# Strassen pairs of a two-layer encoder: where the weight block sums are formed, and the order of the seven products

## The chip, the core and the metric

The kernel runs on one core of one Trainium2 chip. A core has a matrix engine (TensorE, PE in the profile), three engines for elementwise work (VectorE or DVE, ScalarE or ACT, GpSimd or POOL), a sequencer that only issues transfers (SP), and 16 DMA engines that move data between the chip's main memory and the core's on-chip buffers. Each engine works through its own queue in order; semaphores make one wait for another. The metric is the device time of one execution in microseconds (us), the median of several runs.

## What is computed

Two layers over 528 tokens (16 learned meta tokens, then 512 grid tokens) of width 2048, in float32. Each begins with an RMS norm and a large input projection and ends with an output projection added to the residual:

```python
def even_layer(h, ...):
    u = rmsnorm(h, norm_g)
    proj = einsum("bld,de->ble", u, w_in)            # 2048 -> 12352
    y_a = ssd_mixer(...)                             # bidirectional state-space heads
    y_b = conformer_conv(...) * silu(z_b)            # 31-tap convolution channels
    return h + einsum("ble,ed->bld", concat([y_a, y_b]), w_out)   # 4096 -> 2048

def odd_layer(h, ...):
    u = rmsnorm(h, norm_g)
    q, k, v, z = split(einsum("bld,de->ble", u, w_in))            # 2048 -> 8192
    o = neighbourhood_attention(q, k, v, rpb)
    return h + einsum("ble,ed->bld", o * silu(z), w_out)          # 2048 -> 2048
```

A final RMS norm follows, and the meta tokens are dropped.

## The kernel before

Activations are kept transposed: a tile holds 128 channels by 528 tokens. A weight matrix is read in panels of 128 output columns; half a panel is [128 x 8 x 128] floats, 512 KB, one transfer. A float32 product is made of three faster ones: the weight is split into a high part `wh` (ACT, line 196) and a low part `wl` (DVE, line 199), the activations likewise, and each of the eight blocks of 128 rows takes three matmuls (high by high, high by low, low by high). `wh` and `wl` have three buffers each, so the split for a product can begin once the product three before it has left the PE.

Most of the output projections, and the q, k, v projection, are done by Strassen's scheme in Winograd's form. Two panels a and b are a pair; with their upper and lower halves they make the four weight blocks A11, A12 (of a) and A21, A22 (of b), the tokens are cut into two halves, and seven products of 24 matmuls replace eight. On the weights' side this needs four sums,

```python
S1 = A21 + A22;  S2 = S1 - A11;  S3 = A11 - A21;  S4 = A12 - S2
```

which `block_ops` makes on DVE (lines 163, 167, 171). On the activations' side similar combinations (`combos`) are made once a stage: `ta` for products 5 and 7, `tb` for product 6, and a fourth that goes through memory and replaces half of the plain activations for product 4. There are four stages with pairs; each begins with four plain panels (`proj`), during which the combinations are made:

- a: even layer, output projection of the state-space half, 6 pairs;
- b: its convolution half, 6 pairs, added to what a left in memory (`pt_d`);
- c: odd layer, projection to v, q, k, 22 pairs, scaled on POOL (line 823) and stored to `vqk_d`;
- d: odd layer, output projection on 512 tokens, 6 pairs, with the residual.

`sproj` runs the products of a pair: each into its own PSUM tile `pb` (four buffers), then `evac`, the merge, which adds the seven results into the four output blocks, then `fetch` for a coming product. `todo` holds one entry per half panel or product in order; a `fetch` takes the next entry, which issues its load on SP (`load`, line 144) or its sums, and splits one that is there already. Three entries are kept split ahead (`AHEAD`). The products' order is a table: "F" (1, 2, 6, 7, 5, 3, 4) for most pairs, "L" and "E" for the last pair of a stage, with merges of their own (`merge`, and `late` and `early` in stage d).

A scheduler that estimates times sets the order of the rows on each engine's queue, outside the attention part, which is ordered by hand.

Of the kernel before, what the change touches and what calls it, by code (L numbers as in the profile page):

```python
# [12 lines left out]
F32 = mybir.dt.float32  # L13
F32R = mybir.dt.float32r
AF = mybir.ActivationFunctionType
ALU = mybir.AluOpType

P = 128
# [35 lines left out]
ORD = {"F": (1, 2, 6, 7, 5, 3, 4), "L": (1, 2, 4, 3, 6, 7, 5), "E": (4, 6, 7, 5, 1, 2, 3)}  # L54
WOP = {1: "A11", 2: "A12", 3: "S4", 4: "A22", 5: "S1", 6: "S2", 7: "S3"}
NORM = 2
NORMF = 2
PRE = {"F": {0: ("A12", "A21", "A22"), 1: ("S1",)}, "L": {0: ("A12", "A21"), 1: ("S1",), 2: ("S2",)}, "E": {0: ("A21", "S1"), 1: ("S3",), 4: ("A12",)}}
# [17 lines left out]
def hybrid_encoder(ctx: ExitStack, tc: tile.TileContext, hT, win, wdt, wout, oin, oout, par, con,  # L76
# [51 lines left out]
    for seq, last in (([wout[0, (m + 2 * NORM) % KT] for m in range(KT)], "L"), ([wout[1, m] for m in range(KT)], "L"), (vqk, "E")):  # L128
        panels += seq[:2 * NORM]
        for j in range(NORM, len(seq) // 2):  # L130
            panels.append((seq[2 * j], seq[2 * j + 1], last if j == len(seq) // 2 - 1 else "F"))
    panels += [oin[48 + p] for p in range(KT)]
    panels += [oout[m] for m in range(2 * NORMF)]
    for j in range(NORMF, KT // 2):
        panels.append((oout[2 * j], oout[2 * j + 1], "E" if j == KT // 2 - 1 else "F"))
# [11 lines left out]
    def block_ops(pa, pb, order):  # L147
        b = {}

        def get(n):  # L150
            if n in b:
                return b[n]
            if n in ("A11", "A12"):
                r = load(pa, int(n[2]) - 1)
            elif n == "A21":
                r = load(pb, 0)
            elif n == "A22":
                r = load(pb, 1, wx[0], "raw2", 1)
            elif n in ("S1", "S2"):
                x, y, o = ("A21", "A22", ALU.add) if n == "S1" else ("S1", "A11", ALU.subtract)  # L160
                x, y = get(x), get(y)
                r = wx[0].tile([P, KH, P], F32, name=n, tag="sx", bufs=2)
                nc.vector.tensor_tensor(r, x, y, op=o)  # L163
            elif n == "S3":
                get("S1")
                r = get("A21")
                nc.vector.tensor_tensor(r, get("A11"), r, op=ALU.subtract)  # L167
            else:
                y = get("S2")
                r = get("A12")  # L170
                nc.vector.tensor_tensor(r, r, y, op=ALU.subtract)
            b[n] = r
            return r
# [1159 lines left out]
```

## Time and profile before

| | us |
|---|---|
| median of 3 runs | 2707.42 (2706.79 to 2709.77) |
| profiled execution | 2707.44 |
| its span, first to last instruction | 2705.7 |
| PE busy | 2630.5 (97%) |
| PE's weight loads busy | 2508.7 (93%) |
| DVE busy | 2147.2 (79%) |
| ACT busy | 1389.0 (51%) |
| POOL busy | 528.5 (20%) |

Stages a, b and c with their plain panels run from about 1310 to 2175 us, stage d from about 2520 us to the end. Read in the profile: a line of groups gives source line, engine, operation, output and input, count, busy time with the mean in ns, and the idle time of the engine just before with what ended it. A line of waits gives total us, times, and the longest. In the windows, columns are stretch, length, and for each engine busy us with the count of instructions, then the granted PE clock, the share of the DMA engines' time, and GB/s. The PE's matmuls overlap, so its busy time is not its load; the rate of matmuls is.

### The profile page before, as it was taken

How to read it: one execution, taken by the hardware profiler on the slowest of the kernel's cores; microseconds unless marked ns; L12 is line 12 of the kernel's file. 1: busy time of each engine (PE TensorE's matmuls, PEld its weight loads, DVE VectorE, ACT ScalarE, POOL GpSimd, SP SyncE). 2: the span in 40 equal slices, each digit the busy share in tenths (PEclk: the TensorE clock that was granted, in tenths of full speed). 3: DMA queues.
4: the chain of work that ended last, by engine and by line, in shares of the span. 5: the costliest groups of instructions: out<-in, count | busy, mean ns of one | idle time of the engine just before them, and what ended most of it. 6: DMA issues, size and time to landing. Idle time of an engine off the chain costs nothing.

```text
span 2705.7 us, 52618 instructions
## 1 busy us (share of the span) xinstructions
PE 2630.5 (97%) x21228; PEld 2508.7 (93%) x21228; DVE 2147.2 (79%) x2990; ACT 1389.0 (51%) x2567; POOL 528.5 (20%) x568
## 2 busy tenths in 40 slices
PE   8999999999999999999999999999999989999997
PEld 7999999999999999999999999999999967777796
DVE  7775967878587979986888888888888866666886
ACT  5355585665757655225634435533333345655543
POOL 2000000000000001101333532312212242443321
PEclk9999999999999999999999999999999989999998
DMA  4222222222222323434745746633333354444644
GB/s 161 95 76 94 84 74 94 84 94 83 79 90 78 97 77 102 151 128 149 251 141 192 232 150 217 201 130 125 129 132 126 123 154 120 124 131 131 231 161 150
DMA packets 150627, 354.51 MB, mean 131 GB/s; under 512 B 32896, under 2 KB 49408, under 8 KB 150384
## 3 DMA queue, kind: packets, MB, share of 16 engines
q1 hardware_dynamic: 143552, 328.92, 37.8%
q0 software_dynamic: 6544, 22.17, 2.3%
q8 instruction: 166, 2.72, 0.4%
q14 instruction: 77, 0.63, 0.1%
q10 hardware_dynamic: 288, 0.07, 0.0%
HBM read 300.66 MB, written 50.43 MB: 130 GB/s over the span
## 4 chain that ended last, share of the span: by engine, by line
PE 73%; DVE 8%; issue 7%; DMA 5%; ACT 4%; POOL 3%; SPq 0%; DVEq 0%; POOLq 0%; ACTq 0%
PE ps L235 38%; PE pb L216 19%; PE ps L988 7%; DVE wl L199 2%; PE po L974 2%; PE py L506 2%; PE pq L925 1%; PE st L446 1%; ACT wh L196 1%; POOL srt L782 1%; DVE a L529 1%; DVE S L163 1%; DVE raw L167 1%; DMA raw<-oout 1%; DMA raw<-oin 1%
## 5 line engine op out<-in xcount | busy, mean ns | idle before, releaser
L196 ACT ACTIVATE wh<-raw 128x1024 fp32r<-128x1024 f32 (+1 forms) x458 | 484.4, 1058 | 714.2 <-PE pb L216 282.4
L235 PE MATMUL ps<-rh,wh 128*128 128x264 f32 (+2 forms) x3536 | 739.0, 288 | 11.0 <-ACT rh L252 9.2
L235 PE MATMUL ps<-rh,wl 128*128 128x264 f32 (+2 forms) x3536 | 738.9, 288 | 0.2 <-DVE wl L199 0.2
L235 PE MATMUL ps<-rl,wh 128*128 128x264 f32 (+2 forms) x3536 | 734.9, 288 | 1.2 <-DVE rl L253 1.1
L199 DVE TENSOR_TENSOR wl<-raw,wh 128x1024 fp32r<-128x1024 f32 (+1 forms) x458 | 593.3, 1295 | 123.9 <-ACT wh L196 117.7
L235 PEld LDWEIGHTS ps<-rh,wh 128*128 128x128 f32 (+1 forms) x3536 | 554.6, 189 | 17.1 <-ACT rh L252 9.2
L235 PEld LDWEIGHTS ps<-rh,wl 128*128 128x128 f32 (+1 forms) x3536 | 554.0, 189 | 3.4 <-DVE wl L199 0.5
L235 PEld LDWEIGHTS ps<-rl,wh 128*128 128x128 f32 (+1 forms) x3536 | 551.9, 189 | 5.4 <-DVE rl L253 2.0
L216 PE MATMUL pb<-rh,wl 128*128 128x264 f32 (+1 forms) x1280 | 366.9, 287 | 8.7 <-DVE wl L199 8.4
L216 PE MATMUL pb<-rh,wh 128*128 128x264 f32 (+1 forms) x1280 | 365.1, 285 | 3.1 <-ACT wh L196 3.1
L216 PE MATMUL pb<-rl,wh 128*128 128x264 f32 (+1 forms) x1280 | 365.0, 285 | 0.0
L529 DVE SCALAR_TENSOR_TENSOR a<-up,prm,a 128x528 f32<-128x528 f32 x464 | 343.8, 770 | 2.3 <-ACT a L524 0.9
L216 PEld LDWEIGHTS pb<-rh,wl 128*128 128x128 f32 x1280 | 242.2, 189 | 12.4 <-DVE wl L199 12.2
L216 PEld LDWEIGHTS pb<-rh,wh 128*128 128x128 f32 x1280 | 243.0, 190 | 3.7 <-ACT wh L196 3.5
L216 PEld LDWEIGHTS pb<-rl,wh 128*128 128x128 f32 x1280 | 242.7, 190 | 0.0
L216 PE MATMUL pb<-ta,wh 128*128 128x264 f32 (+1 forms) x1280 | 236.4, 285 | 4.6 <-ACT wh L196 4.6
L216 PEld LDWEIGHTS pb<-ta,wh 128*128 128x128 f32 x1280 | 199.1, 189 | 5.7 <-ACT wh L196 5.7
L216 PE MATMUL pb<-ta,wl 128*128 128x264 f32 (+1 forms) x640 | 181.3, 285 | 0.6 <-DVE wl L199 0.4
L196 ACT ACTIVATE wh<-S 128x1024 fp32r<-128x1024 f32 x80 | 84.5, 1057 | 118.7 <-PE pb L216 92.1
L216 PE MATMUL pb<-tb,wh 128*128 128x264 f32 (+1 forms) x640 | 125.5, 293 | 4.4 <-ACT wh L196 3.4
L216 PEld LDWEIGHTS pb<-ta,wl 128*128 128x128 f32 x640 | 120.5, 189 | 1.5 <-DVE wl L199 1.5
L988 PE MATMUL ps<-rh,wh 128*128 128x512 f32 x272 | 114.3, 420 | 0.0
(319 smaller groups left out, 4097.6 us busy)
## 6 DMA issues: line engine op xcount, KB each, us to landing
raw<-win SPq DMA_DIRECT2D x192, 512.0 KB, 3.6
raw<-oin SPq DMA_DIRECT2D x128, 512.0 KB, 3.7
raw<-wout SPq DMA_DIRECT2D x64, 512.0 KB, 4.1
raw<-oout SPq DMA_DIRECT2D x32, 512.0 KB, 3.8
srt<-h_d SPq DMA_DIRECT2D x38, 264.0 KB, 4.6
srt<-yz_d SPq DMA_DIRECT2D x32, 264.0 KB, 4.9
srt<-yb_d SPq DMA_DIRECT2D x32, 264.0 KB, 4.2
vqk_d<-cx SPq DMA_DIRECT2D x26, 264.0 KB, 2.0
```

The costliest lines, as they stand in the source:

```text
L163: nc.vector.tensor_tensor(r, x, y, op=o)
L167: nc.vector.tensor_tensor(r, get("A11"), r, op=ALU.subtract)
L196: nc.scalar.activation(wh, raw, AF.Copy)
L199: nc.vector.tensor_tensor(wl, raw, wh.bitcast(F32), op=ALU.subtract)
L216: nc.tensor.matmul(o, w[:, k, :], u[:, lo:lo + n], start=(k == 0 and j == 0), stop=(k == KH - 1 and j == 2))
L235: nc.tensor.matmul(ps[:M, n, :N], w[:, k, :], u[:, lo + n * N:lo + (n + 1) * N], start=(kk == 0 and j == 0), stop=(kk == KT - 1 and j == 2))
L446: nc.tensor.matmul(st[:, :nd * 256], xb[:, c, 256:], xd[:, d0:d1].rearrange("p r x -> p (r x)"), start=True, stop=True)
L506: nc.tensor.matmul(py[j * HD:(j + 1) * HD, c // 3, (c % 3) * CH:(c % 3 + 1) * CH], a, b, start=(q == 0), stop=(q == nt - 1))
L529: nc.vector.scalar_tensor_tensor(a, u[:, j:j + L], wv(j), a, op0=ALU.mult, op1=ALU.add)
L782: nc.gpsimd.tensor_tensor(r, r, t, op=ALU.add)
L974: nc.tensor.matmul(self.po[hs, w * P:(w + 1) * P], lt, rt, start=(q == 0), stop=(q == nq - 1))
L988: nc.tensor.matmul(ps, w[:, k, :], u[:, lo:lo + S], start=(kk == 0 and j == 0), stop=(kk == KT - 1 and j == 2))
```

## The change

The block sums leave DVE. Two tiles per pair, `wy` (two buffers) and `wx` (one), are loaded by SP and then added to in place by transfers that POOL issues with an addition (`accum_op`): `wy` is A21, then A21 + A22 (product 5), then + A11 (product 6), then + A12 (product 3); `wx` is A11 (product 1), then + A21 (product 7). A12 (product 2) and A22 (product 4) are plain loads. Each addition is issued after the low split that last read the tile (`post`); `wy` of the next pair is started up to three entries early (`EARLY`). Every weight block is so read from memory twice. With all signs plus on the weights' side, signs on the activations' side and in the merges change to match.

The order is the same for every pair, (5, 1, 2, 6, 7, 3, 4), and three products are accumulated onto the PSUM tile of an earlier one: 6 onto 1, 3 onto 5, 4 onto 7, so a pair uses four tiles. The merges shrink: in stages a to c from seven DVE operations and one ACT copy to five and two.

```diff
-ORD = {"F": (1, 2, 6, 7, 5, 3, 4), "L": (1, 2, 4, 3, 6, 7, 5), "E": (4, 6, 7, 5, 1, 2, 3)}
+ORD = (5, 1, 2, 6, 7, 3, 4)
+BANK = {5: "c", 1: "a", 2: "b", 6: "a", 7: "e", 3: "c", 4: "e"}
...
-            elif n in ("S1", "S2"):
-                x, y, o = ("A21", "A22", ALU.add) if n == "S1" else ("S1", "A11", ALU.subtract)
-                x, y = get(x), get(y)
-                r = wx[0].tile([P, KH, P], F32, name=n, tag="sx", bufs=2)
-                nc.vector.tensor_tensor(r, x, y, op=o)
...
+    def block_ops(pa, pb):
+        s = {}
+
+        def half(a, hf):
+            return a[:, hf * KH:(hf + 1) * KH, :]
+
+        def add(n, a, hf):
+            nc.gpsimd.dma_start(s[n], half(a, hf), accum_op=ALU.add)
+
+        def start():
+            s["y"] = load(pb, 0, wx[0], "wy", 2)
+            add("y", pb, 1)
+
+        def left():
+            s["x"] = load(pa, 0, wx[0], "wx", 1)
+            return s["x"]
+
+        return [Entry(lambda: s["y"], start, lambda: add("y", pa, 0)),
+                Entry(left, None, lambda: add("x", pb, 0)),
+                Entry(lambda: load(pa, 1)),
+                Entry(lambda: s["y"], None, lambda: add("y", pa, 1)),
+                Entry(lambda: s["x"]),
+                Entry(lambda: s["y"]),
+                Entry(lambda: load(pb, 1))]
...
+    def take():
+        e = todo.popleft()
+        e.early()
+        pend.append((e.get(), e.post))
+        for e in list(todo)[:EARLY]:
+            if wx[0] is not None:
+                e.early()
...
             nc.vector.tensor_tensor(wl, raw, wh.bitcast(F32), op=ALU.subtract)
             halves.append((wh, wl, M))
+            if post:
+                post()
             if todo:
-                pend.append(todo.popleft()())
+                take()
...
-            ps = wx[1].tile([P, 512], F32, name="pb", tag="pb")
+            new = BANK[b] not in banks
+            if new:
+                banks[BANK[b]] = wx[1].tile([P, 512], F32, name="pb", tag="pb")[:, :n]
...
+                    nc.tensor.matmul(o, w[:, k, :], u[:, lo:lo + n], start=(new and k == 0 and j == 0),
+                                     stop=(k == KH - 1 and j == 2), skip_group_check=not new)
+            evac(b, o, banks)
...
-        def merge(order, x, y):
+        def merge(x, y):
+            def evac(n, p, banks):
+                if n == 1:
+                    nc.scalar.activation(x1, p, AF.Copy)
+                elif n == 2:
+                    vv(x1, x1, p, op=ALU.add)
+                elif n == 6:
+                    nc.scalar.activation(u, p, AF.Copy)
+                    vv(y2, u, banks["c"], op=ALU.add)
                 elif n == 7:
+                    st(y2, y2, -1.0, p, op0=ALU.mult, op1=ALU.subtract)
                 elif n == 3:
                     vv(x2, u, p, op=ALU.add)
+                elif n == 4:
+                    st(y1, u, -1.0, p, op0=ALU.mult, op1=ALU.subtract)
```

How this moves the rows on the engines' queues, at the three places that matter below. On DVE in the middle of stage c, before (S and raw are weight tiles of the block sums, cx, cy and u tiles of the merge):

```order
L163 TENSOR_TENSOR S_22931<-raw,raw_22898 128x1024
L740 TENSOR_TENSOR cx<-u_22769,pb 128x264
L163 TENSOR_TENSOR S_22963<-S_22931,raw 128x1024
L167 TENSOR_TENSOR raw<-raw 128x1024
L199 TENSOR_TENSOR wl<-raw,wh 128x1024
L742 TENSOR_TENSOR cy<-u_22770,pb 128x264
L199 TENSOR_TENSOR wl<-S_22963,wh 128x1024
L171 TENSOR_TENSOR raw<-raw,S_22963 128x1024
```

and now, at such a place:

```order
L203 TENSOR_TENSOR wl<-raw,wh 128x1024
L203 TENSOR_TENSOR wl<-wy,wh 128x1024
L203 TENSOR_TENSOR wl<-wx,wh 128x1024
L717 TENSOR_TENSOR cx<-cx,pb 128x264
L203 TENSOR_TENSOR wl<-wy,wh 128x1024
L203 TENSOR_TENSOR wl<-raw,wh 128x1024
L720 TENSOR_TENSOR cy<-u_23045,pb 128x264
L722 SCALAR_TENSOR_TENSOR cy<-cy,pb 128x264
```

The four sums of a pair are gone, and low splits and merge operations alone are left. On POOL in stage c, before (the scaling of the output tiles of three pairs; the numbers of the tiles are kept):

```order
L823 TENSOR_TENSOR cx_23233<-cx_23233,rs0_84 128x528
L823 TENSOR_TENSOR cy_23234<-cy_23234,rs0_84 128x528
L823 TENSOR_TENSOR cx_23466<-cx_23466,rsa_85 128x528
L823 TENSOR_TENSOR cy_23467<-cy_23467,rs0_84 128x528
L823 TENSOR_TENSOR cx_23699<-cx_23699,rs0_84 128x528
```

and now (wy_23302, wy_23528 and wy_23754 belong to three pairs that follow each other):

```order
L161 DMA wx_23428<-oin 128x1024
L806 TENSOR_TENSOR cy_23270<-cy_23270,rs0_84 128x528
L161 DMA wy_23302<-oin 128x1024
L161 DMA wy_23754<-oin 128x1024
L161 DMA wy_23528<-oin 128x1024
L806 TENSOR_TENSOR cx_23495<-cx_23495,rs0_84 128x528
L161 DMA wx_23654<-oin 128x1024
```

Four adding transfers of each pair stand between the two scalings. On PE at the first pair of stage b, now (pb_17747 is product 2, pb_17684 product 5, pb_17717 product 6 on the tile of product 1):

```order
L224 MATMUL pb_17747<-rh_17030,wh_17600 128x264
L224 MATMUL pb_17747<-rl_17031,wh_17600 128x264
L224 MATMUL pb_17747<-rh_17030,wl_17601 128x264
L224 MATMUL pb_17684<-ta0_17624,wh_17444 128x264
L224 MATMUL pb_17717<-tb0_17166,wh_17709 128x264
L224 MATMUL pb_17717<-tb1_17167,wh_17709 128x264
L224 MATMUL pb_17717<-tb0_17166,wl_17710 128x264
```

Product 5 comes first with 18 matmuls, products 1 and 2 are taken in between, and its last blocks follow here, mixed with product 6.

201 lines of the change are left out of this document (61 added, 140 removed).

## The prediction

> **What bounds the kernel now.** I read the clock first (one core, mean granted 0.986), then the windows of the four stages in which the Strassen pairs run, then what TensorE (PE) waits for there, and last the DMA view. The stages, by their matmuls at line 216, are: a, 6 pairs (first half of the even layer's output projection); b, 6 pairs (second half); c, 22 pairs (the odd layer's q, k, v projections); d, 6 pairs (the odd layer's output projection).
>
> ```profile
> core 0: us, PE busy (x) PEld busy (x) DVE busy (x) ACT busy (x) POOL busy (x), PEclk, DMA share, GB/s
> 1345.00:1481.00 136.00, 128.29 (x1009) 125.35 (x1009) 118.53 (x119) 53.04 (x65) 46.17 (x21) 0.99 0.51 165
> 1528.00:1670.00 142.00, 131.74 (x1008) 129.28 (x1007) 126.16 (x141) 64.94 (x88) 49.79 (x33) 0.95 0.55 178
> 1724.50:2174.00 449.50, 445.48 (x3613) 443.24 (x3613) 382.30 (x398) 170.75 (x185) 93.08 (x43) 1.00 0.40 132
> 2555.00:2685.50 130.50, 122.39 (x1012) 120.42 (x1010) 110.28 (x141) 58.56 (x75) 38.94 (x33) 0.99 0.46 151
> ...
> 1750.00:1800.00 50.00, 50.00 (x411) 50.00 (x411) 43.02 (x45) 18.59 (x19) 10.23 (x5) 1.00 0.40 133
> ```
>
> The last row is a stretch without a gap: 50 us / 411 = 121.7 ns a matmul. A pair has 7 products of 24 matmuls, so a product takes at least 2.92 us and a pair 20.4 us. By that measure stage a needs 6 x 20.4 = 122.6 us and took 136, so 13.4 us are lost; b lost 142 - 122.6 = 19.4 us. In c matmul records are missing, so I count its idle PE: 449.5 - 445.5 = 4.0 us. Stage d has 256 columns in place of 264, 119 us by proportion, so it lost 11.5 us. **About 48 us in all is the ceiling** of what this change can win in the pairs, since it leaves every matmul in place. What the PE waits for (stages a, b, c, d in turn):
>
> ```profile
> PE pb L216 <- DVE wl L199: 7.2, 9, 1.8
> ...
> PE pb L216 <- ACT wh L196: 6.9, 7, 2.4
> PE pb L216 <- DVE wl L199: 3.3, 2, 2.3
> ...
> PE pb L216 <- DVE wl L199: 3.8, 3, 2.5
> ...
> PE pb L216 <- ACT wh L196: 4.3, 4, 2.9
> PE pb L216 <- DVE wl L199: 3.0, 3, 1.1
> ```
>
> It waits for the split weights, and the low half comes from VectorE (DVE), which is 85 to 89% busy in all four. So DVE is the second limit; in c it just fits under the PE.
>
> **What leaves DVE.** The groups of block sums, over all 40 pairs:
>
> ```profile
> L163 DVE TENSOR_TENSOR S<-raw,raw 128x1024 f32<-128x1024 f32 x40 | 50.1, 1253 | 37.9 <-DMA raw<-oin 15.6 <-DMA raw<-wout 10.3 <-DMA raw<-oout 7.4
> L163 DVE TENSOR_TENSOR S<-S,raw 128x1024 f32<-128x1024 f32 x40 | 54.2, 1355 | 0.1
> L167 DVE TENSOR_TENSOR raw<-raw 128x1024 f32<-128x1024 f32 x40 | 81.3, 2033 | 0.0
> L171 DVE TENSOR_TENSOR raw<-raw,S 128x1024 f32<-128x1024 f32 x40 | 81.2, 2031 | 0.1
> L725 DVE TENSOR_TENSOR cx<-u,pb 128x264 f32<-128x264 f32 x33 | 13.7, 416 | 0.0
> L723 ACT ACTIVATE u<-pb 128x264 f32<-128x264 f32 x33 | 12.4, 375 | 3.6 <-PE pb L216 3.6
> ```
>
> The four sums are 50.1 + 54.2 + 81.3 + 81.2 = 266.8 us, 6.7 us a pair. The merge falls from seven DVE operations of 0.42 us to five, 0.8 us more; ScalarE (ACT) gets one more copy of 0.38 us. DVE in c falls from 382.3 to about 382.3 - 22 x 7.5 = 217 us, 48% of the stage; ACT rises by 8 us to 40%. Neither can pace the PE any more. In the DVE rows shown with the change no sum stands between the splits any more; each split of wy or wx waits for a transfer instead, and a late one holds up the merge operation queued behind it.
>
> **What the transfers cost.** SP still issues four 512 KB loads a pair. GpSimd (POOL) issues four adding transfers of 512 KB besides. Its issue is cheap, 5.4 us / 10 = 0.54 us each, 2.2 us a pair, on an engine 21 to 35% busy. The rows that bound the transfer:
>
> ```profile
> L1141 POOL DMA_DIRECT2D rr<-h_d x10 | 5.4, 547 | 0.8 <-POOL fo L1199 0.6 <-DVE rl L1170 0.2
> ...
> raw<-oin SPq DMA_DIRECT2D x85, 512.0 KB, 3.6
> ...
> q1 hardware_dynamic: 143552, 328.92, 37.8%
> ...
> L196 ACT ACTIVATE wh<-raw 128x1024 fp32r<-128x1024 f32 (+1 forms) x458 | 484.4, 1058 | 714.2 <-PE pb L216 282.4 <-PE ps L235 273.7 <-issue 114.3
> L199 DVE TENSOR_TENSOR wl<-raw,wh 128x1024 fp32r<-128x1024 f32 (+1 forms) x458 | 593.3, 1295 | 123.9 <-ACT wh L196 117.7
> ```
>
> No adding transfer is in this trace. Below, it costs a plain load: 3.6 us to land. Above, two loads in a row: 7.2 us. The queue row gives 328.92 MB in 37.8% of 16 engines' 2705.7 us, so 512 KB hold all 16 for 1.63 us of the 3.6; the rest is latency that need not be paid twice. I take one landing and one more stream, **5.2 us**.
>
> How late may it be? Call L the time from the low split that frees wy to the landing of the next sum in it. A split takes 1.06 + 1.30 = 2.4 us. Within a pair wy is split for product 5, added to, split for 6, added to, split for 3; then come the splits of 4 and of the next pair's 5. That chain needs 2 L + 2 x 2.4 + 2 x 1.3 = 2 L + 7.4 us a pair; it stays under the PE's 20.4 us while **L is at most 6.5 us**. A second loop, through the three buffers of split weights (three products, a split, L, a split), needs L + 13.5 us, and binds at 6.9. On POOL the order decides what L holds beside the transfer. In the POOL rows shown with the change, the last addition to one pair's wy (23302), the first to that of the pair after next (23754) and the middle one of the next pair's (23528) follow each other; each waits for a low split or a load, and behind a waiting one stand the scaling of an output tile and its store.
>
> ```profile
> L823 POOL TENSOR_TENSOR cy<-cy,rs 128x528 f32<-128x528 f32 x13 | 28.5, 2193 | 34.9 <-DVE cy L742 34.9
> ...
> raw<-wout SPq DMA_DIRECT2D x64, 512.0 KB, 4.1
> ```
>
> The scaling of cy takes 2.2 us and is ready when the pair's last product ends; the addition behind it is ready a product and a split later (2.9 + 2.4 = 5.3 us). So the POOL work fits in the gap, and in c L is about 5.2 us, 1.3 us inside the bound. In a and b a plain load lands in 4.1 us, so 5.7; two POOL operations of 2.2 us stand in the gap (4.4 of 5.3 us), which leaves less than a microsecond.
>
> **The other edits.** Product 6 now adds onto the bank of product 1, 3 onto that of 5, 4 onto that of 7, so the PE waits for the copy of product 1 (0.38 us on ACT, behind two high splits of 1.06); product 2's 2.9 us hide that, unless the addition to wx lands more than 7.7 us after its split (the copy stands behind that high split). Starting with product 5 asks for all combinations of activations at once; the PE order of stage b (shown with the change) takes 18 of its 24 matmuls, then products 1 and 2, then the rest, which is the cover that products 1 and 2 gave before. I cost both at nothing; uncovered they are a product, 2.9 us, per stage.
>
> **The sum.** Against the profiled execution (span 2705.7, time 2707.44; the median is 2707.42, so no correction). Waits for the low split go, with the matmul slots lost around them: a wins 10 of 13.4; b wins 9 of 19.4, because its 6.9 us for the high split come from the activations' own loads at its start; c wins 3 of 4; d wins 4 of 11.5. That is 26. I take back 6 for additions that land late in a, b and d, a third of a microsecond for each of their 18 pairs. 2707.4 - 20 = **2687 us**; own range 2669 to 2701: down by what is left of a (3.4), c (1) and d (7.5) and no late landings (6), up by b's 9 not won and 5 more of late landings.
>
> **Rivals.**
>
> *The transfers take the place of DVE, and it gets slower (0.34).* If each addition occupies the DMA engines twice, reading both operands in turn, a pair costs them 4 x 2 x 1.63 = 13.0 us more than now. Now it is 0.40 x 20.4 = 8.2 us in c, 0.51 x 22.7 = 11.6 in a, 0.55 x 23.7 = 13.0 in b, 0.46 x 21.75 = 10.0 in d. The sums, 21.2, 24.6, 26.0 and 23.0, exceed today's periods by 0.8 (22 pairs), 1.9, 2.3 and 1.3 us (6 each): 18 + 33 = 51, so 2758 us. It decides from L = 6.5 us on; at L = 7.5 the chain alone makes 22.4 us a pair, 22 x 2 = 44 us in c. Against it: the share counts a packet's waiting as occupation.
>
> ```profile
> GB/s 113 194 245 233 96 255 279 298 146 192 210 90 152 27 180 89 76 136 97 222 283 17 81 219 107 239 245 9 76 220 98 222 285 1 90 275 374 252 304 407
> ```
>
> A fortieth of stage b reached 407 GB/s. At that rate c's 132 GB/s x 20.4 us are 6.6 us and four doubled additions 10.3, 16.9 of 20.4: busy, not full. Hence I keep it second.
>
> The Trainium skill, "Collectives: The Full Stack", section "The bandwidth ceiling: the fold count and why AG ≠ RS ≠ AR", says the addition in a transfer is slow not for the arithmetic but because it needs two source reads, and gives 1.93 as the measured ratio. By that rule this rival's doubling holds and the sum moves towards 2758. No transfer here shows it.
>
> *An addition is as cheap as a load (0.15).* L is 3.6 to 4.1 us, nothing is late, and the stages lose only b's start: 48 - 7 = 41 us, 2666 us.
>
> *DVE was not what the slots waited for (0.13).* The high splits' waits and the starts of stages remain and the late landings take the rest: 2707, within 0.2%.
>
> **Chances.** My forecast has 0.38. A run of this kernel cannot tell less than 0.2% (5.4 us) from no change. Faster: 0.38 and 0.15, less what of the forecast's own range falls within, 0.53. Same: 0.13. Slower: 0.34. The range for 8 in 10 runs from 2656, most of the ceiling, to 2765, just above the slow rival; the likeliest case's own stands above.
>
> **What would show it.** Right: the sums' groups are gone, DVE is near 50% in c, the adding rows land in 5 to 6 us, and stages a and b come to 21 to 22 us a pair with c at 20.4. Wrong: the PE waits for wh, and wh for the adding transfers, in every pair of c; landings of 7 us or more; DMA share near 1 in the four windows. If they land in under 4.5 us, the cheap rival holds. If DVE is relieved and a, b and d keep their periods, the step from DVE's load to the lost slots was wrong.

## The result and the profile after

The changed kernel takes **2857.07 us** (median of 4 runs, 2855.31 to 2858.17) against 2707.4 before: a ratio of 1.055, interval 1.0532 to 1.0569. It is 150 us slower. The forecast was 2687, its range 2656 to 2765: wrong in sign, and outside the range.

The page of the changed kernel, parts 1, 3 and 6 (the numbers after a queue are packets, MB, and share of the 16 DMA engines' time; after an issue, count, size, and median us from issue to landing):

```profile
PE 2666.7 (93%) x21228; PEld 2534.7 (89%) x21228; DVE 1919.4 (67%) x2733; ACT 1392.9 (49%) x2595; POOL 603.6 (21%) x736
...
q0 software_dynamic: 29584, 106.06, 18.7%
...
HBM read 384.55 MB, written 50.43 MB: 152 GB/s over the span
...
raw<-oin SPq DMA_DIRECT2D x84, 512.0 KB, 4.6
wy<-oin POOLq DMA_DIRECT2D x66, 512.0 KB, 6.0
...
wx<-oin POOLq DMA_DIRECT2D x22, 512.0 KB, 7.8
...
DMA to landing us min/median/max: 5.2/7.3/13.4
```

The last row is over all 160 adding transfers. DVE is relieved as the change says, from 79% to 67%. The additions land in 6 to 8 us, where I had 5.2. The four stages of pairs, by windows (columns as in the prediction):

```profile
1342.20:1497.00 154.80, 132.30 (x1010) 129.77 (x1009) 72.64 (x82) 52.69 (x67) 54.65 (x45) 0.94 0.84 214
1545.70:1711.10 165.40, 138.17 (x1009) 134.94 (x1008) 92.53 (x109) 64.46 (x88) 52.94 (x56) 0.92 0.86 222
1762.10:2304.40 542.30, 478.95 (x3697) 468.84 (x3696) 278.68 (x276) 178.56 (x216) 137.31 (x132) 0.97 0.78 194
2683.50:2832.50 149.00, 128.21 (x1008) 125.08 (x1007) 73.95 (x95) 56.48 (x73) 64.24 (x66) 0.95 0.80 208
```

From a stage's first matmul to its last, a takes 154.7 us (136.0 before), b 165.5 (142.1), c 542.3 (459.7) and d 149.0 (130.2): 143.5 of the 150 us. The rest is between the stages. The first pairs of the four stages take 129.7 us together where they took 98.3, so 31 of the 143.5 us are at the stages' starts. What c waits for:

```profile
ACT wh L200 <- DMA wy<-oin: 166.1, 39, 10.8
...
ACT wh L200 <- DMA wx<-oin: 45.6, 19, 4.2
...
PE pb L224 <- DVE cy L720: 35.1, 19, 4.9
```

ScalarE (ACT) waits for the additions, and behind its late split stand its copy of product 6, the merge operation on DVE (line 720) that reads that copy and product 5's tile, and the PE, which may add product 3 onto that tile only after it. Besides, the PE itself waits 25.2 us of c for high splits. POOL's rows of one pair of c, with ACT's three high splits of wy:

```profile
2004.15 0.88 POOL L161 DMA_DIRECT2D wy<-oin  x1 [5.41 <-DVE wl L203]
2015.68 1.74 POOL L161 DMA_DIRECT2D wy<-oin  x2 [10.65 <-DMA wy<-oin]
2017.24 1.54 POOL L806 TENSOR_TENSOR cx<-cx,rsa 128x528 f32<-128x528 f32 x1
2020.17 0.87 POOL L161 DMA_DIRECT2D wx<-oin  x1 [1.40 <-DVE wl L203]
...
2009.54 1.06 ACT L200 ACTIVATE wh<-wy 128x1024 fp32r<-128x1024 f32 x1 [3.45 <-DMA wy<-oin]
2013.42 1.06 ACT L200 ACTIVATE wh<-wy 128x1024 fp32r<-128x1024 f32 x1 [1.36 <-PE pb L224]
2024.62 1.06 ACT L200 ACTIVATE wh<-wy 128x1024 fp32r<-128x1024 f32 x1 [4.08 <-DMA wy<-oin]
```

The last addition (2004.15) is alone and is there at 2009.5. At 2015.68 two follow each other: first the start of the pair after next, which nobody needs yet, then the middle one of the next pair, which product 6 needs; that is there only at 2024.6. Over c, the middle addition takes 8.5 us from its issue to its landing (median), the last one 5.5. (Of a pair's four additions one, wx's, stands between the scaling of cx and that of cy, and three between cy and the next cx.)

### The profile page after: what moved, and what is told of

It reads as the page before. It is cut to its first block, busy times and chain, and to the rows that moved or that the text cites. A ratio compares the mean times of both kernels' runs of the same rounds, so it can differ in the third digit from the quotient of the medians.

```text
span 2854.4 us, 52795 instructions
## 1 busy us (share of the span) xinstructions
PE 2666.7 (93%) x21228; PEld 2534.7 (89%) x21228; DVE 1919.4 (67%) x2733; ACT 1392.9 (49%) x2595; POOL 603.6 (21%) x736
## 3 DMA queue, kind: packets, MB, share of 16 engines
q0 software_dynamic: 29584, 106.06, 18.7%
HBM read 384.55 MB, written 50.43 MB: 152 GB/s over the span
## 5 line engine op out<-in xcount | busy, mean ns | idle before, releaser
L200 ACT ACTIVATE wh<-raw 128x1024 fp32r<-128x1024 f32 (+1 forms) x338 | 356.7, 1055 | 464.1 <-PE ps L243 269.7
L243 PEld LDWEIGHTS ps<-rh,wh 128*128 128x128 f32 (+1 forms) x3536 | 553.3, 189 | 18.7 <-ACT rh L260 9.1
L203 DVE TENSOR_TENSOR wl<-raw,wh 128x1024 fp32r<-128x1024 f32 (+1 forms) x338 | 456.8, 1352 | 114.0 <-ACT wh L200 111.3
L224 PE MATMUL pb<-rh,wh 128*128 128x264 f32 (+1 forms) x1280 | 377.1, 295 | 64.2 <-DVE cy L720 47.8
L203 DVE TENSOR_TENSOR wl<-wy,wh 128x1024 fp32r<-128x1024 f32 x120 | 148.1, 1234 | 244.0 <-ACT wh L200 244.0
L224 PE MATMUL pb<-ta,wh 128*128 128x264 f32 (+1 forms) x1280 | 245.9, 289 | 58.2 <-ACT wh L200 49.2
L200 ACT ACTIVATE wh<-wy 128x1024 fp32r<-128x1024 f32 x120 | 126.8, 1056 | 292.6 <-DMA wy<-oin 166.1
L224 PEld LDWEIGHTS pb<-rh,wl 128*128 128x128 f32 x1280 | 250.4, 196 | 7.9 <-DVE wl L203 7.9
L224 PEld LDWEIGHTS pb<-rl,wh 128*128 128x128 f32 x1280 | 250.8, 196 | 0.0
L203 DVE TENSOR_TENSOR wl<-wx,wh 128x1024 fp32r<-128x1024 f32 x80 | 130.2, 1628 | 113.4 <-ACT wh L200 113.4
L200 ACT ACTIVATE wh<-wx 128x1024 fp32r<-128x1024 f32 x80 | 84.6, 1058 | 229.5 <-PE pb L224 128.8
```

Source lines behind the costliest of these rows:

```text
L200: nc.scalar.activation(wh, raw, AF.Copy)
L203: nc.vector.tensor_tensor(wl, raw, wh.bitcast(F32), op=ALU.subtract)
L224: nc.tensor.matmul(o, w[:, k, :], u[:, lo:lo + n], start=(new and k == 0 and j == 0), stop=(k == KH - 1 and j == 2), skip_group_check=not new)
L243: nc.tensor.matmul(ps[:M, n, :N], w[:, k, :], u[:, lo + n * N:lo + (n + 1) * N], start=(kk == 0 and j == 0), stop=(kk == KT - 1 and j == 2))
```

## The experiments

Stage times (first to last matmul of the pairs), and in c the mean period of pairs 2 to 21, all read from the traces. Ratios are to runs of the kernel before on the same chip.

| run | us | ratio, interval | a | b | c | d | pair in c |
|---|---|---|---|---|---|---|---|
| before | 2707 | 1 | 136.0 | 142.1 | 459.7 | 130.2 | 20.7 |
| the change | 2857 | 1.055 [1.0532, 1.0569] | 154.7 | 165.5 | 542.3 | 149.0 | 24.1 |
| e1 in order | 2808 | 1.0374 [1.0353, 1.0395] | 154.5 | 158.0 | 504.7 | 145.7 | 22.4 |
| e2 copies | 2728 | 1.0078 [1.0053, 1.0102] | 133.5 | 146.7 | 471.7 | 129.7 | 20.9 |
| e3 order, sums on DVE | 2748 | 1.015 [1.0133, 1.0167] | 140.7 | 146.2 | 471.9 | 145.2 | 20.8 |
| e4 no sums | 2657 | 0.9813 [0.9799, 0.9828] | 123.0 | 131.0 | 451.9 | 121.7 | 20.5 |
| e5 half | 2706 | 1.0001 [0.9989, 1.0012] | 127.6 | 141.3 | 465.1 | 125.8 | 20.7 |
| e6 sum on POOL | 2776 | 1.0252 [1.0232, 1.0273] | 149.2 | 149.4 | 509.8 | 139.1 | 22.9 |
| e7 nobody waits | 2973 | 1.098 [1.0962, 1.0998] | 172.6 | 206.1 | 581.5 | 122.5 | – |
| e8 old order, two | 2703 | 0.9986 [0.9977, 0.9995] | 138.5 | 138.4 | 458.3 | 133.4 | 20.5 |
| e9 order, no sums | 2685 | 0.9921 [0.9905, 0.9937] | 124.2 | 130.8 | 460.0 | 122.7 | 20.7 |
| e10 chain two | 2874 | 1.0615 [1.059, 1.064] | 158.1 | 171.5 | 540.1 | 150.7 | 24.1 |
| e11 sum later | 2686 | 0.9914 [0.9897, 0.993] | 132.6 | 134.0 | 454.8 | 126.8 | 20.5 |
| e12 store on POOL | 2681 | 0.9896 [0.988, 0.9912] | 129.8 | 127.3 | 457.3 | 127.9 | 20.5 |
| e13 start sooner | 2842 | 1.0502 [1.0476, 1.0528] | 165.7 | 163.2 | 529.4 | 152.8 | 23.6 |
| e14 own tile | 2865 | 1.0579 [1.0554, 1.0604] | 151.1 | 163.9 | 556.8 | 148.5 | 25.1 |
| e15 spread | 2823 | 1.0423 [1.0404, 1.0441] | 154.8 | 160.1 | 518.8 | 144.1 | 23.1 |
| e16 spread, PE | 2817 | 1.0404 [1.0387, 1.0421] | 155.0 | 159.1 | 515.7 | 142.1 | 22.9 |

### e1: the additions in the program's order

```diff
-            nc.gpsimd.dma_start(s[n], half(a, hf), accum_op=ALU.add)
+            if adds:
+                with tc.issue_after(adds[-1].ins):
+                    adds.append(nc.gpsimd.dma_start(s[n], half(a, hf), accum_op=ALU.add))
+            else:
+                adds.append(nc.gpsimd.dma_start(s[n], half(a, hf), accum_op=ALU.add))
```

> The changed kernel with its adding transfers issued on POOL in the order of the program: the first addition to a pair's wy no longer stands ahead of the middle addition of the pair before it. Everything else is as in the changed kernel. Theory Q (the place on the queue makes the middle addition late, 8.9 us instead of 5.7): both additions inside a pair land in about 5.7 us, the chain is 2 x 5.7 + 7.4 = 18.8 us and fits under the PE's 20.4; stage c falls from 542 us to 455-475 and the whole to 2700-2750 us. Theory D (each addition reads twice and the DMA engines are the limit, whatever the order): c stays above 520 us, DMA share in c at 0.8 or more, the whole 2830-2860. Theory M (the accumulation in place and the one order of products cost the time): no change, 2845-2865.

49 us come back, 38 of them in c, where the middle addition now lands 5.4 us after its issue (median) in place of 8.5. No forecast holds: Q wanted 2700 to 2750, D and M 2830 and more. POOL's order is about a third of the loss.

### e2: copies in place of additions

```diff
-            nc.gpsimd.dma_start(s[n], half(a, hf), accum_op=ALU.add)
+            nc.gpsimd.dma_start(s[n], half(a, hf))
```

> The changed kernel with every adding transfer turned into a plain copy of the same 512 KB from the same place, on the same queue, in the same order, with the same waits; the block sums are left out, so products 5, 6, 7 and 3 use single blocks. Theory D (the doubled reads): a copy lands in 3.6-4.5 us instead of 5-9, DMA share in c falls from 0.81 to about 0.6, c comes to 455-475 us and the whole to 2690-2735. Theory Q (the place on POOL's queue): the landings get shorter but the middle copy still stands behind the first one of the next pair; c keeps more than half of its 83 us, the whole 2770-2840. Theory M: 2840-2860.

129 us less than the changed kernel, within D's range, though a copy lands in 5.2 us in the median and not in the 3.6 to 4.5 that D gave it. Its queue row and its issues:

```profile
q0 software_dynamic: 29584, 106.06, 11.7%
...
L161 POOL DMA_DIRECT2D wy<-oin x66 | 36.0, 548 | 320.3 <-DVE wl L203 164.2 <-DMA wy<-oin 155.6 <-issue 0.4
```

Packets and bytes are those of the additions, and so is what is read from HBM, the chip's main memory (384.55 MB), but they hold the engines 11.7% of 2722.8 us, 319 us, in place of 18.7% of 2854.4, 534 us. Without the share that was there before (2.3% of 2705.7, 62 us) that is 257 against 472: an addition holds the engines 1.8 times as long. Packet by packet, 4 KB of an addition take 328 ns in the median, 4 KB of a plain transfer 159. So the longer hold is not more reading from main memory. That it is the reading of the tile that is added to, which lies on the chip, fits, but no row shows it. The issue costs POOL 0.55 us for a copy and 0.88 for an addition.

### e3 and e9: the order, the accumulation and the merges alone

e3 keeps the new order with sums on DVE; e9 leaves sums and additions out.

```diff
 e3 (sketch; each one product ahead of its use)
+    b["S"] = A21 + A22;  b["S"] += A11;  b["A21"] += A11;  b["A12"] += b["S"]   # all on DVE
 e9
-            nc.gpsimd.dma_start(s[n], half(a, hf), accum_op=ALU.add)
+            pass
```

> The other half of the change alone: one order (5, 1, 2, 6, 7, 3, 4), accumulation onto three earlier tiles and the smaller merges, while the four block sums are made by DVE from plain loads again (S1 and S2 in one tile, two buffers for A22), each one product ahead of its use. No adding transfer is left. Theories Q and D (the additions cost the time): 2690-2725 us, c at 455-470 us with DVE at 80-85% there, no adding row in the trace. Theory M (the order and the accumulation cost it): above 2780, the PE waiting for ACT's copies and DVE's merge operations.

> The changed kernel with its additions simply left out: the new order, the accumulation in place and the new merges, only the four plain loads a pair, no sums. Against the old order without sums (2657) it is the price of the order, the accumulation and the merges alone; against the run with plain copies (2728) it is the price of 4 x 512 KB more a pair on POOL's queue. Theory O (the order costs, by its stage starts, c's end and 0.2 us a pair): 2685-2715. Theory X (the order costs nothing; the extra transfers cost the 71 us between 2657 and 2728): 2655-2670.

The part that I had costed at nothing costs time: e9 is 28 us slower than e4 (described next), which leaves out the same sums in the old order, and e3 41 us slower than the kernel before, between its two forecasts. Two places are seen. A steady pair takes 20.7 us in place of 20.5. e9's rows around the start of product 3 (PE; then DVE):

```profile
1923.28 0.28 PE L224 MATMUL pb<-ta,wl 128*128 128x264 f32 x1
1923.53 0.39 PE L224 MATMUL pb<-rh,wh 128*128 128x264 f32 x1
1923.76 0.29 PE L224 MATMUL pb<-rl,wh 128*128 128x264 f32 x1
...
1921.91 1.23 DVE L203 TENSOR_TENSOR wl<-raw,wh 128x1024 fp32r<-128x1024 f32 x1 [1.94 <-ACT wh L200]
1923.06 0.42 DVE L720 TENSOR_TENSOR cy<-u,pb 128x264 f32<-128x264 f32 x1
```

The steps there are 0.25 and 0.23 us in place of 0.12: product 3 adds onto product 5's tile and waits until DVE has read it (1923.06 to 1923.48), which comes after a low split. The rest is at the ends of c: its first pair takes 25.1 us (21.2 in e4), and from its end to the start of d it is 379 us in place of 369 (378 to 380 in every run with the new order, 369 to 372 in those with the old); why, no run shows. In a, b and d, e3's pairs take 24 us; I did not pursue that.

### e4: the sums left out, old order

```diff
...
-                nc.vector.tensor_tensor(r, x, y, op=o)
-            elif n == "S3":
+            elif n in ("S1", "S3"):
+                get("A22")
+                r = get("A21")
+            elif n == "S2":
                 get("S1")
-                r = get("A21")
-                nc.vector.tensor_tensor(r, get("A11"), r, op=ALU.subtract)
+                r = get("A11")
             else:
-                y = get("S2")
+                get("S2")
                 r = get("A12")
-                nc.vector.tensor_tensor(r, r, y, op=ALU.subtract)
```

> The kernel before with its four block sums left out: the same loads, tiles, orders of products and merges, and the products take the plain blocks in place of S1 to S4. It frees DVE of 266.8 us and adds nothing: the price of DVE's share by itself. Theory R (the prediction's: the lost matmul slots wait for DVE): a, b, c, d win about 10, 9, 3 and 4 us, the whole 2675-2690. Theory N (DVE is not what they waited for, since the copies without sums won nothing): within 5 us of before, 2700-2711.

Better than R's forecast: 51 us less than before.

```profile
1342.50:1465.50 123.00, 123.00 (x1009) 123.00 (x1009) 79.95 (x89) 52.93 (x63) 37.49 (x21) 1.00 0.52 174
1512.30:1643.40 131.10, 126.86 (x1010) 125.99 (x1009) 97.08 (x122) 66.15 (x88) 38.05 (x32) 0.97 0.61 197
1694.20:2146.30 452.10, 451.69 (x3699) 451.48 (x3698) 290.39 (x321) 176.21 (x193) 59.91 (x60) 1.00 0.41 136
2515.50:2637.30 121.80, 119.99 (x1009) 119.52 (x1008) 83.02 (x117) 57.49 (x74) 35.99 (x33) 0.99 0.50 165
```

Every pair but the first of a stage now takes 20.5 us in a to c and 19.6 in d. The sums on DVE were what most lost slots waited for: 40 us come back in the stages, and 7 to 10 outside them. The run takes out two things at once, DVE's work and the step that a sum puts between a load and its split (in the kernel before ACT waits 26.6 us in all for S), and does not part them.

### e5 and e10: two additions outside the chain, two inside

In e5 S1 and S3 stay adding transfers; DVE makes the sums for 6 and 3 in place. e10 is the reverse.

```diff
 e5
+        def s2():
+            nc.vector.tensor_tensor(s["y"], s["y"], s["x"], op=ALU.add)
+            add("x", pb, 0)
...
 e10
+        def s1():
+            nc.vector.tensor_tensor(s["y"], s["y"], s["t"], op=ALU.add)
...
+        def s3():
+            nc.vector.tensor_tensor(s["x"], s["x"], s["t"], op=ALU.add)
...
```

> The changed kernel with two of its four additions taken back to DVE: S1 (A21 + A22, begun early) and S3 (A11 + A21) stay adding transfers, in the program's order on POOL; the sums for products 6 and 3 are made by DVE in place from tiles that are on the chip anyway (A11 and A12). The chain through wy then holds no transfer between the products 5, 6 and 3, and 2 x 512 KB a pair are read a second time instead of 4 x. Theory C (the chain of two late additions inside a pair sets the period): c near the 472 us of the run with DVE sums, the whole 2740-2760. Theory D (DMA engines' share): half of the 81 us between the in-order run (2808) and the copies (2728), 2760-2785.

> The counterpart to the run with S1 and S3 as adding transfers (2706): here S1 and S3 are made by DVE from one more plain load each, and the two additions inside wy, for products 6 and 3, stay adding transfers. So two adding transfers a pair again, but both in the chain, where a split waits for them. Theory C (the chain): most of the 102 us between 2706 and the in-order run (2808) returns, 2770-2810, c above 495 us. Theory D (the number of doubled reads): near 2706 plus the two extra loads and 3.3 us a pair of DVE, 2715-2750.

Stage c, e5 above, e10 below, then what the PE and DVE wait for in e10's c:

```profile
1710.10:2175.30 465.20, 459.57 (x3698) 454.75 (x3697) 335.45 (x319) 182.22 (x215) 98.36 (x89) 0.99 0.64 177
...
1770.60:2310.70 540.10, 480.28 (x3698) 474.67 (x3697) 312.54 (x319) 177.42 (x213) 127.42 (x90) 0.95 0.71 196
...
PE pb L237 <- DVE cy L733: 54.2, 21, 5.4
...
DVE wy L172 <- DMA raw<-oin: 44.0, 20, 3.0
```

e5 is level with the kernel before and beats even C's range; e10 is the slowest of all that compute the whole function, beyond C's 2810 and slower than with four additions, though it has two and its DMA engines are 71% busy in c against 78%. Its two additions never overlap. So two additions a pair are not too many by themselves (e5), and too much traffic is not what makes e10 slow. How much of e10's loss is the chain's is not shown: its additions land 5.5 (middle) and 6.8 us (last) after their issue, and in its c DVE also stands still 44.0 us, ahead of splits and merge operations, for one of the two more plain loads (line 172), while all that the PE waits for is a merge operation of DVE.

### e6: one sum on POOL

```diff
...
-                nc.vector.tensor_tensor(r, get("A11"), r, op=ALU.subtract)
+                nc.gpsimd.tensor_tensor(r, get("A11"), r, op=ALU.subtract)
```

> The kernel before with one of the four sums, S3 = A11 - A21, on POOL instead of DVE in the common order of products, asked for one product earlier; DVE gives up 2.0 us a pair. By POOL's 2.2 us for 528 columns it takes 4.3 us there. Theory R: a third of the 26 us, 2695-2700. Theory N: 2703-2710; worse than 2710 if the sum on POOL comes late for product 7 or stands ahead of POOL's scaling.

69 us slower. "Worse than 2710" came, but not for the reasons given: no engine waits for the sum on POOL, and what the PE waits for in c are DVE's low splits (38.8 us). The groups in e6:

```profile
L163 DVE TENSOR_TENSOR S<-S,raw 128x1024 f32<-128x1024 f32 x40 | 121.9, 3047 | 0.1
...
L167 POOL TENSOR_TENSOR raw<-raw 128x1024 f32<-128x1024 f32 x40 | 97.6, 2441 | 436.2 <-DVE S L163 264.7 <-ACT wh L196 171.5
```

POOL takes 2.44 us for the sum, but DVE's S2 rises from 1.36 to 3.05, and its splits of S from 1.25 to 1.68. What DVE gave up it lost again.

### e7: the additions to a scratch tile

```diff
-            nc.gpsimd.dma_start(s[n], half(a, hf), accum_op=ALU.add)
...
+            z = zsc[0]
...
+                    adds.append(nc.gpsimd.dma_start(z, half(a, hf), accum_op=ALU.add))
```

> The changed kernel in the program's order on POOL with each adding transfer of stages a, b and c pointed at one scratch tile that nothing reads (one after another, each 512 KB read and added); the products take the plain loaded blocks, so the sums are left out; in stage d the additions are left out altogether. Same traffic, no split waits for it. Theory D (the DMA engines are the limit): the plain loads come late instead, c stays above 500 us, plain loads land in 6 us or more, the whole 2775-2810. Theory C (the chain of late landings is what costs, not the traffic): a, b and c at the copies' 134, 147 and 472 us, the whole 2710-2735.

Inconclusive. Each addition waited for the one before on POOL's queue (166.1 us in a stretch of 230), the scalings of the output waited behind them, SP's stores for those, and the weight loads behind the stores. Its slow pairs (31 to 34 us in b) measure that, not the traffic.

### e8, e11, e12: the old order with two additions

e8 is e5's division of the sums with the old orders and merges. In e8 alone product 2 of the last pairs of c and d took S4 in place of A12. e11 sets that right and moves S2 behind a split; e12 is e11 with stage a's stores moved to POOL.

```diff
 e8
+        def s2():
+            b["S2"] = wp.tile([P, KH, P], F32, name="S2", tag="raw", bufs=3)
+            nc.vector.tensor_tensor(b["S2"], b["y"], b["x"], op=ALU.add)
...
 e11
-        S4 = E("A12", [(1, s4)])
+        S4 = E("A12", [(0 if order == "E" else 1, s4)])
...
-        x1 = E("x", first + [(0, s2)], ax)
+        x1 = E("x", first, lambda: (s2(), ax()))
 e12
-            nc.sync.dma_start(pt_d[k], t)
+            nc.gpsimd.dma_start(pt_d[k], t)
```

> A mix: the products' orders and the merges of the kernel before (signs as in the changed kernel), S1 and S3 made by adding transfers in the program's order on POOL, S2 and S4 by DVE (S2 into a tile of its own, S4 in place). DVE gives up 3.3 us a pair, no transfer stands between products 6 and 3, and 2 x 512 KB a pair are read a second time. If the in-place chain, the order of products and the doubled reads of the other two additions are what the changed kernel loses, this comes near the kernel without sums (2657): steady pairs at 20.5-20.8 us in c and the whole 2660-2690, faster than both. If two additions a pair already load the DMA engines too much, or one of them is late for product 7, it stays within 5 us of the kernel before or above, 2702-2730.

> The mix of old order and two adding transfers with one thing moved: S2 on DVE comes behind the first product's low split instead of ahead of it, so DVE no longer stands still for a late load of A11 (18.6 us of waits in stage a, 9.9 in d of the mix); the addition of A21 into wx starts 1.4 us later. If those waits set the pairs of 24-25 us in a and d, a falls from 138.5 to about 128 and d from 133 to about 126, c keeps 20.5 a pair, the whole 2680-2695. If the loads are late for another reason (SP's stores ahead of them wait for POOL), 2697-2707.

> The same, and stage a's stores of its sums to memory are issued by POOL, which makes them, instead of SP, where they waited 41.6 us for POOL with the weight loads queued behind them. If that queue is what makes a's loads late: a at 124-127, b earlier by the same, 5-12 us less than the run it is sent with. If not, the same time within 2 us.

e8 has its steady pairs of c at 20.5 but lost that at a's and d's loads, so it fell into its second range. e11 gets 17 us of it, within its forecast for the whole. e12 gets another 5; the intervals of e11 and e12 overlap, so the 5 are not certain, and a came to 129.8, not to the 124 to 127 forecast. **e12 is faster than both kernels: 0.9896 of the one before.** Its stages:

```profile
1343.90:1473.80 129.90, 125.95 (x1010) 124.91 (x1010) 105.59 (x103) 53.61 (x65) 55.66 (x44) 0.99 0.80 220
1525.30:1652.70 127.40, 124.14 (x1010) 123.26 (x1009) 107.33 (x125) 62.41 (x83) 45.70 (x40) 1.00 0.82 241
1703.60:2161.00 457.40, 453.38 (x3697) 452.96 (x3697) 349.88 (x366) 176.53 (x194) 114.92 (x102) 1.00 0.68 183
2531.50:2659.50 128.00, 122.41 (x1009) 120.38 (x1008) 99.14 (x133) 58.69 (x77) 44.46 (x46) 0.99 0.73 210
```

A DMA share of 0.80 stands beside a granted clock of 0.99 in a: the share alone does not make a stage slow.

### e13 to e16: can four additions be placed well?

e13 and e15 both start from e1. e13 begins the next pair's wy sooner, and e14 is e13 with product 3 in a tile of its own. e15 holds the start back a product by a one-column copy on POOL, and e16 is e15 with the PE's products pinned in the program's order.

```diff
 e13
-EARLY = 3
+EARLY = 6
 e14
-BANK = {5: "c", 1: "a", 2: "b", 6: "a", 7: "e", 3: "c", 4: "e"}
+BANK = {5: "c", 1: "a", 2: "b", 6: "a", 7: "e", 3: "d", 4: "e"}
...
 e15
...
+                adds.append(nc.gpsimd.tensor_copy(t, wl[:, 0, :1].bitcast(F32)))
...
 e16
+            with (tc.issue_after(mms[-1].ins) if b in (6, 7, 3) else ExitStack()):
```

> The in-order run with one number changed: the next pair's wy is begun six entries ahead instead of three, so its first addition follows the middle one (which has two products' time) on POOL's queue and no longer comes 0.9 us behind the last one (which has one product's). Same four additions, same bytes. Theory C (late landings in the chain; in the in-order run the last addition took 8.2 us, shared with the next pair's first): the last one lands in 5.7-6.5 us, c falls from 505 to 470-490 us, the whole from 2808 to 2740-2785. Theory D (four doubled reads a pair are too many wherever they stand): c stays at 500-510, the whole 2800-2815.

> The same, and product 3 gets a PSUM tile of its own instead of adding onto that of product 5, so the PE no longer waits there for VectorE to have read product 5, which stands behind ACT's copy of product 6 and that behind the split that waits for the last addition; the merge keeps its five operations on DVE (stages a to c; one more in d). If the accumulation in place makes late landings dearer (27.6 us of waits for that merge operation in the in-order run's c), c falls by another 5-25 us, the whole by 10-40; if it only takes the 0.24 us a pair that the order without sums shows there, 5-10 us; if the PE waits for the splits anyway, 0-3.

> The in-order run with its four additions spread: the first addition to the next pair's wy is held back by a copy of one column on POOL that reads the low split of product 7, so it comes a product after the last addition instead of 0.9 us behind it. In the traces an addition lands 5.4-5.6 us after its issue when none is before it, and 3.3-4.7 us after the one before when it is behind one. Theory S (they are served one after another, and an urgent one that meets another is what is late): the last lands in 5.4-5.8 us instead of 6.2 (up to 8.2), c falls from 505 to 470-490 us, the whole from 2808 to 2750-2785. Theory D (four doubled reads a pair are too many wherever they stand): 2800-2815. If the held-back addition is now late for its own split: above 2815.

> The same, and the PE's products kept in the order 5, 1, 2, 6, 7, 3, 4: the scheduler had set one or two matmuls of product 7 ahead of product 6, so the PE asked for the sum in wx a product earlier. If that was a second urgent addition: 5-30 us less than the run it is sent with. If the last addition alone decides: the same within 5 us.

All four miss what I hoped, and theories C and S, as I had put them, fell: none comes below e1. Theory D, that four additions a pair are too many wherever they stand, is not refuted by any of them, though e13, e14, e15 and e16 lie above its range too. In e15 the start is late for its own split: in c the split for product 5 waits 61.9 us for additions, where it waits 40.3 in e1 and not at all in the change or e13. e13 shows why moving one does not help. Its POOL and ACT rows of one pair in c:

```profile
2084.95 1.74 POOL L164 DMA_DIRECT2D wy<-oin  x2 [10.80 <-DVE wl L208]
...
2089.44 0.88 POOL L164 DMA_DIRECT2D wx<-oin  x1 [1.39 <-DVE wl L208]
...
2094.25 0.88 POOL L164 DMA_DIRECT2D wy<-oin  x1 [2.58 <-DVE wl L208]
...
2097.60 1.06 ACT L205 ACTIVATE wh<-wx 128x1024 fp32r<-128x1024 f32 x1 [4.91 <-PE pb L229]
2101.61 1.07 ACT L205 ACTIVATE wh<-wy 128x1024 fp32r<-128x1024 f32 x1 [2.67 <-DMA wy<-oin]
```

By the trace's landings these four land at 2090.5, 2093.5, 2097.5 and 2101.5: the first 5.6 us after its issue, each other 3 to 4 us after the one before. The last, issued 5 us after the third, is still behind it. Over c, an addition with none before it lands 5.4 to 5.7 us after its issue in the change, e1 and e15 (6.6 in e13, and 6.3 in e10, where none ever meets another); one that is issued while another is under way lands 3.4 to 5.0 us after that one (a copy in e2 1.9). In every run with four of them in a pair most are issued while another is under way (61 of c's 85 in the change).

Why that is dear, by L, medians in c over pairs 2 to 21. L is read here from the end of the low split that frees wy to the start of the next high split of it, so it also holds what else that split waited for:

| | change | e1 | e2 | e10 | e13 | e14 | e15 | e16 |
|---|---|---|---|---|---|---|---|---|
| L, middle addition | 10.0 | 6.1 | 7.0 | 8.6 | 7.4 | 6.5 | 5.9 | 5.9 |
| L, last addition | 5.9 | 6.2 | 5.2 | 7.3 | 8.1 | 8.8 | 6.7 | 6.7 |
| both + 7.4 | 23.3 | 19.7 | 19.6 | 23.3 | 22.9 | 22.7 | 20.0 | 20.0 |
| last + 15.8 | 21.7 | 22.0 | 21.0 | 23.1 | 23.9 | 24.6 | 22.5 | 22.5 |
| median period | 23.9 | 21.9 | 20.7 | 24.2 | 23.4 | 25.1 | 22.8 | 22.8 |

The first sum is the prediction's chain. For the second it had L + 13.5, which falls short; 15.8 is fitted to these runs, not derived. The larger of the two is within 0.9 us of each period. That describes the runs and does not prove the chain: L is itself a stretch of the period, and in e10 1.7 us of the middle L come after the landing. If the fit holds, the last addition may take 4.7 us for 20.5 a pair, and the shortest landing of an addition in the change is 5.2 us; but the 0.5 us between them are less than the fit's own error, and it was made in one order of products, so whether some place for the four could have paid stays open. e14 took away the PE's waits for the merge operation (17.9 us in 470 us of e13's c) and got more for the high splits (58.0 in place of 24.8). With the longer waits came a lower clock: over all of c, the matmuls that ran while the granted clock stood at 0.5 cost 29 us more than 121.7 ns each in e14, 13 in e13, so 16 of the 27 us between them. e16 pins product 7's first matmuls behind product 6; its interval overlaps with e15's, so nothing follows.

## Why the prediction was wrong

The loss is divided by runs, along one path of several: the sums gone give 51 us (2707 to 2657, e4); the order, accumulation and merges take 28 (to 2685, e9); four more loads a pair, for which splits wait, 43 (to 2728, e2); the additions' longer hold 129 (to 2857), of which POOL's order is 49 (e1). By another path the parts differ: with the sums still on DVE, the order, accumulation and merges take 41 (e3).

- *DVE is what the lost slots wait for.* Right as far as the sums go, and too low: I took 26 of 48; e4 won 13.0 in a, 11.1 in b, 7.8 in c, 8.5 in d, and more outside the pairs. Rival "DVE was not the cause" is refuted.
- *About 48 us is the ceiling; in c records are missing.* Misread: no record is missing. My window of c ended at 2174, and the last of its 3696 matmuls is at 2184. The stage takes 459.7 us, 9.9 more than 22 x 168 matmuls at 121.7 ns, where I had 4.0; the ceiling by the prediction's measure is 54.
- *DVE falls to 217 us in c.* It fell to 278.7 (from 390.6 over the whole stage). The sums' rows held time that belongs to POOL's neighbourhood (last section); it moved to the splits, whose row for wx stands at 1.63 us.
- *L is about 5.2 us in c, 1.3 us inside the bound of 6.5.* **This step failed.** To the landing, as the prediction counts it, the middle addition's L is 9.9 us and the last one's 5.8 (medians in c); the two plus 7.4 make 23.1 us a pair, over the PE's 20.4, and the period was 23.9. The size of one transfer was nearly right: one landing and one more stream gave 5.2, which is the minimum, and an addition with none ahead lands in 5.7. What failed is that I gave every addition this landing, as if it were alone: 61 of c's 85 are issued while another is under way, and land 7.7 us after their issue (median).
- *The POOL work fits in the gap.* **Failed too.** I saw the start of the pair after next between two urgent additions and asked only whether POOL had time for it, not what it does to the issue and the landing of the one behind it: 49 us (e1).
- *The bound on L (6.5, and 6.9 from the second loop).* The first loop alone does not hold: e1's two L give 19.7 us, and its pairs take 21.9. By the fit above the second has some 2.3 us more in it than I counted; what they are, no run shows. Neither loop has the wait of product 5's split, which is 40.3 us of c in e1.
- *The other edits at nothing.* Failed: 28 us. I had named the merge's cover, not the PE's wait for DVE on product 5's tile nor the ends of c.
- *The rival with doubled transfers (2758).* Its doubling is right: the engines are held about twice as long. Its limit is not what the trace shows, since the engines are 78% busy in c. By the Trainium skill ("Collectives: The Full Stack", section "The bandwidth ceiling: the fold count and why AG ≠ RS ≠ AR") two source reads give 1.93, measured there between two collectives; the trace has 2.06 by packets and 1.8 by share, and it agrees in size. Its price was 99 us short: it added up shares of the engines' time, left the chain as an alternative instead of a further term, and left out the order's 28 us.
- *What would show it.* The marks for "wrong" came: wh waits for the adding transfers, and landings of 7 us. The DMA share near 1 did not; it is 0.78 to 0.86.

## What to carry to other kernels

Before work is moved from an engine to transfers, ask for each transfer who waits for it and how many products it has to land. Here two additions with several products' time to land left the steady pairs of c at the PE's 20.5 us and, with the old order, won 1% (e12), while every run with additions between consecutive splits of one tile was 3.7 to 6.2% slower than the kernel that has the sums on the engine. The latency of a transfer measured alone is a floor: on POOL's queue here each one landed 3.4 to 5.0 us after the one before it, and an urgent one paid for each that stood ahead of it.

## What the runs showed of the hardware

A DVE operation on two operands in SBUF, the on-chip buffer of the tiles, that runs beside a POOL tensor operation takes longer: in c of the changed kernel, DVE's low splits that overlap with one take 2.28 us on average (44 of them) and the others 1.22 (111); in e6's c its splits and sums take 2.32 (87) and 1.22 (133). The Trainium skill, "SBUF — State Buffer", section "Who interferes with whom", says that a DVE instruction with two SBUF inputs contends with a GpSimd instruction that reads SBUF; these rows agree. I had read the in-place sums' 2.03 us as the price of a sum; in the kernel before, the 61 of the 80 that overlap with a POOL tensor operation take 2.29 us and the other 19 take 1.22.

After a long wait the PE often pays a second time. In e14, windows around one stall of 3.2 us:

```profile
1915.00:1923.00 8.00, 8.00 (x68) 8.00 (x67) 3.66 (x4) 2.12 (x2) 3.24 (x3) 1.00 1.05 219
1923.00:1928.00 5.00, 2.06 (x13) 1.84 (x12) 1.18 (x2) 1.33 (x2) 0.00 (x0) 0.85 0.98 230
1928.00:1930.50 2.50, 2.50 (x15) 2.50 (x14) 0.83 (x3) 1.06 (x1) 0.00 (x0) 0.61 0.50 156
1930.50:1936.00 5.50, 5.50 (x48) 5.50 (x47) 3.45 (x5) 2.40 (x3) 0.00 (x0) 1.00 0.54 168
```

After it the granted clock is 0.61 for 2.5 us and 15 matmuls run there, where 20 fit at 121.7 ns. The clock's own rows stand at 0.5 for 3.4 us from 1926.6, and the matmuls in them are 0.22 us apart. Not every wait is followed by this: in the same c, one of 3.1 us is followed by a clock of 1.00. Over the four stages such matmuls cost about 35 us more than 121.7 ns each in the change and 10 in the kernel before, so some 25 of its 143.5 us are slower matmuls and not waits.
